# A streaming Huber loss: three pairs of 32 KiB-per-partition tiles replaced by two pairs of 48 KiB-per-partition tiles

## The chip, the core and the metric

The kernel runs on one core of one Trainium2 chip. The metric is the device time of one execution in microseconds (us); lower is better. Beside the times of repeated executions there is a profile of one execution, with a record of every instruction on every engine and of every packet that the core's 16 DMA engines moved. Engine names are those of the profile: DVE is VectorE, ACT is ScalarE, POOL is GpSimd, and SP is SyncE, which here only issues transfers ("SPq" is its instruction queue).

## The reference

Two fp32 matrices of 8192 x 8192 go in and one of the same size comes out. Every element is computed by itself:

```python
def reference(pred, target):
    delta = 1.0
    diff = pred - target
    abs_diff = np.abs(diff)
    return np.where(abs_diff <= delta, 0.5 * diff**2, delta * (abs_diff - 0.5 * delta))
```

There is no reduction and no reuse: 256 MiB of `pred` and 256 MiB of `target` are read once, 256 MiB are written once, 805.3 million bytes in all.

## The kernel before

**Tiling.** The 8192 rows are cut into 64 blocks of 128 rows. In block `i` each of the 128 partitions holds one row of 8192 fp32 elements, which is 32 KiB per partition and 4 MiB per transfer. A tile `a` receives `pred`, a tile `b` receives `target`, and the result is computed in place: `a` ends up holding the output and is the source of the store. Three pairs of `a` and `b` rotate (`DEPTH = 3`), 6 x 32 = 192 KiB per partition.

**Arithmetic.** The whole tile is loaded by two transfers, but computed in four pieces of 2048 columns. For one piece, `first` issues two DVE instructions (the difference `a = a - b`, line 58; the difference clipped to -1..1 into `b`, line 59) and three ACT instructions (`a = |a|`, line 62; `a = relu(a - 1)`, line 63; `b = b*b`, line 64). `second` issues one more DVE instruction (`a = 0.5*b + a`, line 69). Since ACT needs what DVE made and line 69 needs what ACT made, a piece's `second` is put into DVE's order two pieces later: a list `late` holds the pieces that are waiting. The list lives across tiles. So the last two pieces of tile `i` get their `second` only after the `first` of two pieces of tile `i + 1`, and DVE, which runs its instructions in order, can issue those only when tile `i + 1` has landed.

**Order of the transfers.** All transfers are issued by SP, in one program order, on one hardware queue. The order is written out by hand (`manual_schedule` for SP, DVE and ACT). Three tiles are loaded at the start: b, a, b, a, b, a. From then on, when the last `second` of tile `j` has been issued, SP gets the store of tile `j` (line 53) and then the loads of tile `j + 3` into the same pair: `b` (line 49), then `a` (line 50). Three waits follow from the buffers: the store waits for line 69 of the tile's last piece; the load of `b` waits for that tile's compute alone; the load of `a` waits until the store of the same buffer has landed, and everything behind it on SP waits with it.

**End.** The last tile is loaded in two halves (four transfers of 2 MiB) and stored in four pieces of 1 MiB, each as soon as its `second` is through. The tile before it is stored whole.

Of the kernel before, what the change touches and what calls it, by code (L numbers as in the profile page):

```python
# [1 line left out]

# [4 lines left out]

P = 128
ROW = 8192
PIECE = 2048  # L10
DEPTH = 3


@with_exitstack
def kernel(
    ctx: ExitStack,
    tc: tile.TileContext,
    pred: bass.AP,
    target: bass.AP,
    out: bass.AP,  # L20
):
    nc = tc.nc
    f32 = mybir.dt.float32
    Alu = mybir.AluOpType
    Act = mybir.ActivationFunctionType
    Eng = mybir.EngineType

    pred_t = pred.rearrange("(n p) m -> n p m", p=P)
    targ_t = target.rearrange("(n p) m -> n p m", p=P)
    out_t = out.rearrange("(n p) m -> n p m", p=P)  # L30
    n = pred_t.shape[0]
    H = ROW // 2

    const = ctx.enter_context(tc.tile_pool(name="const", bufs=1))
    pool_a = ctx.enter_context(tc.tile_pool(name="pool_a", bufs=DEPTH))
    pool_b = ctx.enter_context(tc.tile_pool(name="pool_b", bufs=DEPTH))

    neg1 = const.tile([P, 1], f32)
    nc.vector.memset(neg1, -1.0)  # L39

    A, B = {}, {}

    def load(i, halves):


        A[i] = pool_a.tile([P, ROW], f32, name="a")
        B[i] = pool_b.tile([P, ROW], f32, name="b")
        for lo, hi in halves:
            nc.sync.dma_start(out=B[i][:, lo:hi], in_=targ_t[i, :, lo:hi])  # L49
            nc.sync.dma_start(out=A[i][:, lo:hi], in_=pred_t[i, :, lo:hi])  # L50

    def store(i, lo, hi):
        nc.sync.dma_start(out=out_t[i, :, lo:hi], in_=A[i][:, lo:hi])

    def first(i, lo, hi):

        a, b = A[i][:, lo:hi], B[i][:, lo:hi]
        nc.vector.tensor_tensor(out=a, in0=a, in1=b, op=Alu.subtract)  # L58
        nc.vector.tensor_scalar(  # L59
            out=b, in0=a, scalar1=-1.0, scalar2=1.0, op0=Alu.max, op1=Alu.min  # L60
        )
        nc.scalar.activation(out=a, in_=a, func=Act.Abs)  # L62
        nc.scalar.activation(out=a, in_=a, func=Act.Relu, bias=neg1)  # L63
        nc.scalar.activation(out=b, in_=b, func=Act.Square)  # L64

    def second(i, lo, hi):

        a, b = A[i][:, lo:hi], B[i][:, lo:hi]
        nc.vector.scalar_tensor_tensor(  # L69
            out=a, in0=b, scalar=0.5, in1=a, op0=Alu.mult, op1=Alu.add  # L70
        )

    whole = [(0, ROW)]
    split = [(0, H), (H, ROW)]
    pieces = [(lo, lo + PIECE) for lo in range(0, ROW, PIECE)]

    with tc.manual_schedule(engines={Eng.SP, Eng.DVE, Eng.Activation}):
        for i in range(DEPTH):
            load(i, whole)
        late = []  # L80
        for i in range(n):
            for k, (lo, hi) in enumerate(pieces):
                first(i, lo, hi)
                late.append((i, lo, hi))
                if len(late) > 2:
                    j, l, h = late.pop(0)
                    second(j, l, h)
                    if h == ROW and j < n - 1:
                        store(j, 0, ROW)
                        if j + DEPTH < n:  # L90
                            load(j + DEPTH, split if j + DEPTH == n - 1 else whole)
                    elif j == n - 1:
                        store(j, l, h)
        for j, l, h in late:
            second(j, l, h)
            store(j, l, h)


# [1 line left out]
_INS = ['pred', 'target']  # L100
_OUTS = [((8192, 8192), 'float32')]


# [23 lines left out]
```

## Time and profile before

| What | Value |
|---|---|
| Median of 3 executions | 1875.93 us (1875.44 to 1877.06) |
| The profiled execution's own time | 1875.44 us |
| Its span in the profile | 1873.7 us |
| DVE busy | 1446.7 us, 77% of the span |
| ACT busy | 1447.2 us, 77% of the span |
| Transfers of SP's queue | 805.32 MB, their packets fill 99.9% of the 16 engines' span |
| Mean rate | 430 GB/s |
| Transfers issued | 189 of 4 MiB, 4 of 2 MiB, 4 of 1 MiB |

How to read it: the span runs from the first to the last record of the profiled execution and is 1.7 us shorter than its time. "Busy" is the time in which an engine executed something, not what an engine could do. The share of the DMA queue is the time that its packets took, divided by 16 engines' spans. A rate over a slice of the span is the bytes of the packets in it over its length. In groups of instructions, the idle time is that of the engine just before the instruction, with the releaser that ended it.

### The profile page before, as it was taken

The page shows a single profiled execution, that of the slowest core. Times are in us where ns is not written, and L with a number is a line of the kernel's source. Part 1 is how long each engine was busy: PE and PEld are TensorE (multiplying, and loading weights), DVE is VectorE, ACT ScalarE, POOL GpSimd, SP SyncE. Part 2 cuts the span into 40 slices and gives each one's busy share as a digit, 9 for nine tenths or more (in the row PEclk, how much of TensorE's full clock was granted, in tenths as well). Part 3 has the DMA queues.
Part 4 walks back from the last instruction along what each step waited for, and adds up shares of the span by engine and source line. Part 5 has one row for each costly group of instructions (what it writes and reads, how often), then busy time and mean ns, then how long its engine had stood idle before and what let it go on. Part 6 is the DMA issues. An engine that isn't in the chain of part 4 may idle for free.

```text
span 1873.7 us, 1976 instructions
## 1 busy us (share of the span) xinstructions
DVE 1446.7 (77%) x769; ACT 1447.2 (77%) x769; POOL 0.2 (0%) x4
## 2 busy tenths in 40 slices
DVE  4986877878778778787787877878778787787777
ACT  4986877878778787787877878778778787787877
POOL 0000000000000000000000000000000000000000
DMA  9999999999999999999999999999999999999998
GB/s 414 425 435 430 432 433 432 432 433 432 433 435 430 433 434 431 432 434 432 432 434 431 432 434 432 432 434 432 434 434 431 434 433 432 432 434 434 431 411 373
DMA packets 28384, 805.45 MB, mean 430 GB/s; under 512 B 3152, under 2 KB 3152, under 8 KB 3152
## 3 DMA queue, kind: packets, MB, share of 16 engines
q1 hardware_dynamic: 28368, 805.32, 99.9%
q14 instruction: 16, 0.13, 0.0%
HBM read 536.87 MB, written 268.44 MB: 430 GB/s over the span
## 4 chain that ended last, share of the span: by engine, by line
DMA 74%; DVE 20%; issue 3%; ACT 2%; ACTq 0%; SPq 0%; DVEq 0%
DMA out_dram<-a 44%; DMA a<-in_pred_dram 30%; DVE a L58 8%; DVE a L69 8%; DVE b L59 4%; ACT a L62 1%; ACT b L64 1%; ACT a L63 1%; ACTq L122 0%; DVEq L58 0%; SPq L49 0%; SPq L50 0%
## 5 line engine op out<-in xcount | busy, mean ns | idle before, releaser
L58 DVE TENSOR_TENSOR a<-a,b 128x2048 f32<-128x2048 f32 x256 | 585.2, 2286 | 405.7 <-DMA a<-in_pred_dram 353.9
L62 ACT ACTIVATE a<-a 128x2048 f32<-128x2048 f32 x256 | 488.8, 1909 | 382.9 <-DVE b L59 382.9
L69 DVE SCALAR_TENSOR_TENSOR a<-b,a 128x2048 f32<-128x2048 f32 x256 | 584.8, 2285 | 1.4 <-ACT b L64 1.4
L63 ACT ACTIVATE a<-a,neg_64 128x2048 f32<-128x2048 f32 x256 | 512.5, 2002 | 8.3
L64 ACT ACTIVATE b<-b 128x2048 f32<-128x2048 f32 x256 | 484.7, 1893 | 0.0
L59 DVE TENSOR_SCALAR b<-a 128x2048 f32<-128x2048 f32 x256 | 314.1, 1227 | 8.8
L62 ACT ACT_TABLE_LOAD x1 | 1.3, 1283 | 22.7 <-DMA a<-in_pred_dram 22.7
L39 DVE MEMSET neg_64<- 128x1 f32 x1 | 0.1, 59 | 0.8 <-PEq L111 0.8
L111 POOL MEMSET const-bfloat16-1.0<- 128x1 bf16 x1 | 0.1, 102 | 0.0
L111 POOL MEMSET const-uint8-127<- 128x1 uint8 x1 | 0.1, 102 | 0.0
L111 POOL MEMSET const-float32-1.0<- 128x1 f32 x1 | 0.1, 99 | 0.0
L111 POOL MEMSET const-float32-0.0<- 128x1 f32 x1 | 0.1, 98 | 0.2 <-issue 0.2
## 6 DMA issues: line engine op xcount, KB each, us to landing
b<-in_target_dram SPq DMA_DIRECT2D x63, 4096.0 KB, 36.5
a<-in_pred_dram SPq DMA_DIRECT2D x63, 4096.0 KB, 19.4
out_dram<-a SPq DMA_DIRECT2D x63, 4096.0 KB, 27.2
b<-in_target_dram SPq DMA_DIRECT2D x2, 2048.0 KB, 23.0
a<-in_pred_dram SPq DMA_DIRECT2D x2, 2048.0 KB, 15.0
out_dram<-a SPq DMA_DIRECT2D x4, 1024.0 KB, 10.3
```

What stands on the lines that cost most here:

```text
L39: nc.vector.memset(neg1, -1.0)
L58: nc.vector.tensor_tensor(out=a, in0=a, in1=b, op=Alu.subtract)
L59: nc.vector.tensor_scalar(out=b, in0=a, scalar1=-1.0, scalar2=1.0, op0=Alu.max, op1=Alu.min)
L62: nc.scalar.activation(out=a, in_=a, func=Act.Abs)
L63: nc.scalar.activation(out=a, in_=a, func=Act.Relu, bias=neg1)
L64: nc.scalar.activation(out=b, in_=b, func=Act.Square)
L69: nc.vector.scalar_tensor_tensor(out=a, in0=b, scalar=0.5, in1=a, op0=Alu.mult, op1=Alu.add)
L111: nc = _bacc.Bacc("TRN2", target_bir_lowering=False, num_devices=1)
```

## The change

The two inputs and the output are flattened and cut into contiguous blocks of 128 x 12288 elements: 48 KiB per partition and 6 MiB per transfer. 67,108,864 elements make 42 such blocks and a last one of 128 x 8192, so there are 43 tiles in place of 64. `DEPTH` is 2: two pairs of 48 KiB tiles, 4 x 48 = 192 KiB per partition as before. A piece is still 2048 columns, so a tile has six pieces (the last tile four), and every arithmetic instruction has the shape it had and occurs 256 times.

The list `late` is now made anew for each tile and emptied at the tile's end: all six `second` of tile `i` stand in DVE's order ahead of the first `first` of tile `i + 1`. The store of tile `i` follows them, then the loads of tile `i + 2` into the same pair. The last tile is loaded in two halves of 4096 columns (2 MiB each) and stored in four pieces, as before. SP issues 126 transfers of 6 MiB, 4 of 2 MiB and 4 of 1 MiB, 134 in place of 197. SP's waits are of the same kinds as before.

```diff
-ROW = 8192
+ROW = 12288
 PIECE = 2048
-DEPTH = 3
+DEPTH = 2
...
-    pred_t = pred.rearrange("(n p) m -> n p m", p=P)
-    targ_t = target.rearrange("(n p) m -> n p m", p=P)
-    out_t = out.rearrange("(n p) m -> n p m", p=P)
-    n = pred_t.shape[0]
-    H = ROW // 2
+    total = pred.shape[0] * pred.shape[1]
+    flat = [x.rearrange("r c -> (r c)") for x in (pred, target, out)]
+
+    tiles = []
+    at = 0
+    while at < total:
+        w = min(ROW, (total - at) // P)
+        tiles.append((at, w))
+        at += P * w
+    n = len(tiles)
+
+    def dram(x, i):
+        at, w = tiles[i]
+        return flat[x][at : at + P * w].rearrange("(p m) -> p m", p=P)
...
+    def cuts(w, step):
+        return [(lo, min(lo + step, w)) for lo in range(0, w, step)]
+
-    def load(i, halves):
+    def load(i):
         A[i] = pool_a.tile([P, ROW], f32, name="a")
         B[i] = pool_b.tile([P, ROW], f32, name="b")
-        for lo, hi in halves:
-            nc.sync.dma_start(out=B[i][:, lo:hi], in_=targ_t[i, :, lo:hi])
-            nc.sync.dma_start(out=A[i][:, lo:hi], in_=pred_t[i, :, lo:hi])
+        w = tiles[i][1]
+        for lo, hi in cuts(w, w // 2 if i == n - 1 else w):
+            nc.sync.dma_start(out=B[i][:, lo:hi], in_=dram(1, i)[:, lo:hi])
+            nc.sync.dma_start(out=A[i][:, lo:hi], in_=dram(0, i)[:, lo:hi])
 
     def store(i, lo, hi):
-        nc.sync.dma_start(out=out_t[i, :, lo:hi], in_=A[i][:, lo:hi])
+        nc.sync.dma_start(out=dram(2, i)[:, lo:hi], in_=A[i][:, lo:hi])
...
     with tc.manual_schedule(engines={Eng.SP, Eng.DVE, Eng.Activation}):
         for i in range(DEPTH):
-            load(i, whole)
-        late = []
+            load(i)
         for i in range(n):
-            for k, (lo, hi) in enumerate(pieces):
+            w = tiles[i][1]
+            late = []
+            for lo, hi in cuts(w, PIECE):
                 first(i, lo, hi)
-                late.append((i, lo, hi))
+                late.append((lo, hi))
                 if len(late) > 2:
-                    j, l, h = late.pop(0)
-                    second(j, l, h)
-                    if h == ROW and j < n - 1:
-                        store(j, 0, ROW)
-                        if j + DEPTH < n:
-                            load(j + DEPTH, split if j + DEPTH == n - 1 else whole)
-                    elif j == n - 1:
-                        store(j, l, h)
-        for j, l, h in late:
-            second(j, l, h)
-            store(j, l, h)
+                    second(i, *late[0])
+                    if i == n - 1:
+                        store(i, *late[0])
+                    late.pop(0)
+            for lo, hi in late:
+                second(i, lo, hi)
+                if i == n - 1:
+                    store(i, lo, hi)
+            if i < n - 1:
+                store(i, 0, w)
+                if i + DEPTH < n:
+                    load(i + DEPTH)
```

More of the change, by code (lines that the diff above doesn't have):

```diff
@@ L71, in second @@
         )
-    whole = [(0, ROW)]
-    split = [(0, H), (H, ROW)]
-    pieces = [(lo, lo + PIECE) for lo in range(0, ROW, PIECE)]
     with tc.manual_schedule(engines={Eng.SP, Eng.DVE, Eng.Activation}):
         for i in range(DEPTH):
-            load(i, whole)
-        late = []
+            load(i)
         for i in range(n):
-            for k, (lo, hi) in enumerate(pieces):
+            w = tiles[i][1]
+            late = []
+            for lo, hi in cuts(w, PIECE):
                 first(i, lo, hi)
-                late.append((i, lo, hi))
+                late.append((lo, hi))
                 if len(late) > 2:
-                    j, l, h = late.pop(0)
-                    second(j, l, h)
-                    if h == ROW and j < n - 1:
-                        store(j, 0, ROW)
-                        if j + DEPTH < n:
-                            load(j + DEPTH, split if j + DEPTH == n - 1 else whole)
-                    elif j == n - 1:
-                        store(j, l, h)
-        for j, l, h in late:
-            second(j, l, h)
-            store(j, l, h)
+                    second(i, *late[0])
[10 more added lines that the diff above has]
+                    load(i + DEPTH)
 _INS = ['pred', 'target']
```

## The prediction

> **What bounds the kernel now.** I read the page first: engines, rates and the queue.
>
> ```profile
> span 1873.7 us, 1976 instructions
> DVE 1446.7 (77%) x769; ACT 1447.2 (77%) x769; POOL 0.2 (0%) x4
> ...
> DMA  9999999999999999999999999999999999999998
> GB/s 414 425 435 430 432 433 432 432 433 432 433 435 430 433 434 431 432 434 432 432 434 431 432 434 432 432 434 432 434 434 431 434 433 432 432 434 434 431 411 373
> ...
> q1 hardware_dynamic: 28368, 805.32, 99.9%
> ```
>
> DVE and ACT idle for a quarter of the span, the DMA engines never: 431 to 435 GB/s in nearly every slice. So the transfers are the bound, their bytes stay the same, and only two things can move the time: the rate while the queue is full, and stretches in which it runs empty.
>
> Next the windows of one 4 MiB round each (29.06 us), at the end of the run, where the queue empties:
>
> ```profile
> 1760.49:1789.55 29.06, 22.60 (x13) 22.59 (x13) 0.00 (x0) 1.00 1.00 433
> 1789.55:1818.61 29.06, 22.63 (x13) 22.63 (x13) 0.00 (x0) 1.00 1.00 430
> 1818.61:1847.67 29.06, 28.89 (x16) 28.90 (x16) 0.00 (x0) 1.00 0.96 389
> 1847.67:1868.50 20.83, 14.31 (x8) 13.40 (x8) 0.00 (x0) 1.00 0.97 416
> ```
>
> The last column is GB/s: a full round moves 430 to 433, the last stretches 389 and 416. The loss against 432.5 is 29.06 x 43.5/432.5 + 20.8 x 16.5/432.5 = 3.7 us; on the slowest DMA engine, whose landings decide, the trace has 2.3 us of it.
>
> Then the timeline of all engines over the first tile (start, duration, instruction), and that of SP's queue in a steady stretch.
>
> ```profile
> 0.73 0.38 SPq L49 DMA_DIRECT2D b<-in_target_dram  x1
> ...
> 22.72 2.29 DVE L58 TENSOR_TENSOR a<-a,b 128x2048 f32<-128x2048 f32 x1 [21.86 <-DMA a<-in_pred_dram]
> ...
> 26.31 1.91 ACT L62 ACTIVATE a<-a 128x2048 f32<-128x2048 f32 x1 [2.33 <-DVE b L59]
> ...
> 37.60 1.89 ACT L62 ACTIVATE a<-a 128x2048 f32<-128x2048 f32 x1
> ...
> 53.59 0.35 SPq L53 DMA_DIRECT2D out_dram<-a  x1
> ```
>
> ```profile
> 1705.51 0.33 SPq L50 DMA_DIRECT2D a<-in_pred_dram  x1
> 1707.37 0.34 SPq L53 DMA_DIRECT2D out_dram<-a  x1
> ...
> 1734.59 0.33 SPq L50 DMA_DIRECT2D a<-in_pred_dram  x1
> ```
>
> Line 50 is issued the moment a store lands: 1705.51, 1734.59, so every 29.08 us, 9.69 us per 4 MiB transfer. The first pair lands at 22.7 us; a piece takes ACT 5.64 us (two from 26.31 to 37.60); the first store goes out at 53.59, before the sixth load ends (6 x 9.7 + 3.3 = 61.5). Three pairs keep the queue full from the start.
>
> **The change part by part.** The sum is made against the profiled execution (1875.44 us, span 1873.67) and raised by 0.5 us to the median. All on the slowest DMA engine.
>
> *Bytes and packets.* By the packet records a 32768-byte packet takes 1.213 us, 16384 bytes 0.611, 8192 bytes 0.309: a line of 36.8 ps per byte and 8 ns per packet. Nothing more is visible per transfer: 8 packets per engine are 9.70 us, the landings 9.69 us apart. A 49152-byte packet is then 1.816 us and a 6 MiB transfer 14.51 us. Before: 189 x 9.693 = 1832.0 us. After: 126 x 14.51 = 1828.3. **-3.7 us.** Bounds: 0, if the longer rows bring nothing; -10, if everything ran at the best slice's 435 GB/s (805.3/0.435 = 1851.3 us against 1832.0 + 4 x 4.88 + 4 x 2.43 = 1861.2); +12 at the slices' 430. I take the packet line, measured on the operation itself.
> The Trainium skill speaks here for the change and against it. "SBUF — State Buffer", section "The DMA setup-cost knee", gives each transfer a fixed 2 us or so; 63 fewer would be -126 us and a sum near 1775. The row of landings shows no such cost while the queue is full. "DMA: Bandwidth & Descriptors", section "Where 436 GB/s comes from", sets a ceiling of 435.2 GB/s, by which no transfer size could give more than some 11 us; by it the sum would be 1890 at best.
>
> *The start.* Only two pairs are loaded ahead. The first pair lands 2 x (14.51 - 9.69) = 9.6 us later than 22.7, at 32.3; the second has its last byte in at 61.0 and lands at 61.3. Computing a tile of six pieces: ACT starts 3.59 us after DVE (26.31 - 22.72), works 6 x 5.64 = 33.9, the last line 69 takes 2.29: 39.8 us, and SP issues 0.05 later. So store 0 is issued at 72.2. Its first bytes move 1.1 us after issue (first packets of the run: 1.80 against 0.73), at 73.3. The queue behind it holds only loads that need this store's or this compute's buffers, so all 16 engines stand still from 61.0 to 73.3: **+12.3 us, and 0.7** for slow first packets (1.4 to 2.1 us in place of 1.2 when the queue fills from empty). Nothing hides it: three pairs did. Bounds: 11 (if packets move at once on issue) to 14.5 (2.6 us between issue and landing beyond transfer, 22.72 - 0.73 - 19.39, all of it ahead).
>
> *The steady rounds.* Per tile the transfers take 3 x 14.51 = 43.5 us, the compute 39.8. Counted from the last byte of tile i's `a`: 0.35 to landing (packet end to semaphore), 0.1 to DVE, 39.85, 1.1 to the store's first bytes = 41.4. Tile i+1's last byte is in at 43.5. The store arrives **2.1 us early**, and behind it the next `b` (14.5 us) covers the wait of `a` for the store's landing. So 0. With the whole 2.6 us above taken ahead of the bytes, the margin is 0.9. DVE and SP meanwhile wait in order: no `first` of tile i+1 passes the emptying of `late`, but that tile has not landed anyway.
>
> *The end.* Take E as the last byte of tile 41's `a`. Store 40 (14.5) and the four 2 MiB loads (4 x 4.87) keep the queue until E+34.0. Store 41 waits for tile 41's compute: first bytes at E+41.4, **idle 7.4, and 0.7** to restart; in until E+56.6. Tile 42 starts on DVE at E+40.3. Its `second`s follow the order p0 p1 p2 s0 p3 s1 s2 s3 and ACT's 5.64 us steps: the four stores are issued at E+53, 58.7, 63.2 and 68.8. Each moves 2.43 us, so the queue waits 0.7, 2.1 and 3.2 us more; end at E+72.3, against 58.2 of transfers: **+14.1 us**. Before, three pairs let the last tile's first half land under the compute of the tile ahead, and the same stretch lost 2.3. Net **+11.8**. Bounds: 9 (bytes move at once on issue, which takes 1.1 off, and 3.7 lost before) and 14 (what was lost before is lost again).
>
> *Arithmetic, issues.* The same 256 instructions of each kind by the same rows; 63 fewer issues of 0.4 us on SP, which waits most of the span: 0. Memory stays at 192 KiB per partition.
>
> **Sum:** -3.7 + 13.0 + 11.8 = +21.1: profiled 1896.5, median 1897.0 us, 1.1% slower.
>
> **The rivals.**
>
> 1. *The steady cover is too short.* If the store comes x us after the last byte of the next tile, two tiles share one such chain, so each round grows by x/2; 40 rounds make 20 us per us. For: the margin is only 2.1 us of 43.5, and the landings of one transfer differ by 0.4 us between engines early and up to 6.3 late. Against: the slowest engine's own landing starts the compute and its own queue is what must not run dry; the others idling costs nothing. With x = 1: 1917 us; if half of the 6.3 counted (x = 1): the same; if all of it (x = 4.2): 1981.
>
> 2. *6 MiB blocks stream slower*, for their rows or addresses in memory: at 430 GB/s 15.7 us above my sum (12 + 3.7), 1913. Nothing in the profile speaks for it but the spread of its slices.
>
> 3. *Not slower: longer rows stream faster.* The two gaps cost 24.8 us. To pay for them a 49152-byte packet must save 24.8/1008 = 25 ns against 1.5 x 1.212 us: 1.793 us, 438.6 GB/s. From there on the change isn't slower; at 441 GB/s it would be 1866. Against: no slice of 40 is over 435, and three packet sizes lie on one line. For: no packet of this size is in the trace.
>
> 4. *The rows are not moved as 48 KiB packets* but are cut (32 + 16): the change then doesn't do what it says, and -3.7 becomes 0: 1900.7.
>
> **How the numbers follow.** My forecast together with rival 4: 0.73, its own range 1889 to 1904 from the bounds of its terms. Rival 1: 0.13, mostly 1905 to 1925. Rival 2: 0.06. Rival 3: 0.08, of it 0.05 faster and 0.03 within 0.2% (3.8 us, about what a measurement of this kernel can tell from no change). So slower by over 0.2%: 0.92. The range 1886 to 1916 holds nearly all of the first, half of rivals 1 and 2, and leaves the rest out.
>
> **What would show it.** In the profile after: the DMA share falls in the second of the 40 slices (some 13 of 46.8 us) and in the last two, and stays at 9 between, at 432 to 434 GB/s. SP's first store is issued near 72, its line for `a` every 43.5 us. DVE's wait for `a` is some 3.7 us per tile. ACT and DVE keep their busy sums. Wrong would be: rounds above 44 us with a DMA share below 1 inside them (rival 1), or with a full share (rival 2); rounds under 43.2 (rival 3); about 33300 data packets in place of 17152 (rival 4); or a first store before 65 us.

## The result, and the profile after

The changed kernel takes 1917.91 us (median of four executions, 1916.55 to 1919.87); the kernel before took 1876.49 us in the same comparison. The ratio is 1.0221, 95% interval 1.0203 to 1.0239: **2.2% slower**, 41 us, where 21 us had been forecast.

The page of the changed kernel, the same parts as were shown of before:

```profile
span 1914.8 us, 1891 instructions
...
DVE 1452.6 (76%) x769; ACT 1440.0 (75%) x769; POOL 0.2 (0%) x4
...
DMA  9799999999999999999999999999999999999996
GB/s 416 307 426 429 437 431 428 427 435 418 438 416 428 439 414 438 417 440 419 422 427 430 424 427 428 427 440 414 439 421 437 424 429 426 429 425 419 435 416 279
...
q1 hardware_dynamic: 19296, 805.31, 98.4%
```

DVE and ACT do what they did. The gap at the start (second slice, 307 GB/s) and the one at the end (279) are where the prediction put them. What it did not have is between: the engines are busy in every slice (9), but the rate averages less than the 432 to 433 of before. The swing from 414 to 440 is mostly the page's counting. It puts a packet's bytes whole into the slice in which the packet starts, and 16 packets of 48 KiB are 16 GB/s of a slice of 47.9 us; spread over the packets' times, the records give 423 to 433 in these slices. The windows of the changed kernel by stage say how much is lost (last two columns: DMA share, GB/s):

```profile
0.00:61.00 61.00, 27.79 (x17) 25.51 (x14) 0.20 (x4) 1.00 0.97 413
61.00:74.00 13.00, 7.42 (x4) 9.50 (x6) 0.00 (x0) 1.00 0.14 60
...
134.60:1841.40 1706.80, 1313.40 (x695) 1304.23 (x697) 0.00 (x0) 1.00 1.00 428
1841.40:1875.50 34.10, 31.41 (x17) 30.07 (x17) 0.00 (x0) 1.00 0.93 387
1875.50:1883.50 8.00, 4.66 (x3) 3.66 (x2) 0.00 (x0) 1.00 0.23 98
1883.50:1914.80 31.30, 20.68 (x12) 22.51 (x12) 0.00 (x0) 1.00 0.73 310
```

The kernel before, over its middle and over one stretch of it:

```profile
134.60:1818.60 1684.00, 1304.55 (x694) 1304.37 (x694) 0.00 (x0) 1.00 1.00 432
379.00:1790.00 1411.00, 1091.86 (x580) 1091.45 (x580) 0.00 (x0) 1.00 1.00 433
```

The middle 1707 us of the changed kernel have a DMA share of 1.00 and 428 GB/s. At 432.5 the same bytes would take 1689 us. So some 18 us were lost with the DMA engines busy. SP's queue in the changed kernel shows it from another side, in the steps from store to store (line 66):

```profile
1704.69 0.34 SPq L66 DMA_DIRECT2D out_dram<-a  x1
...
1749.34 0.34 SPq L66 DMA_DIRECT2D out_dram<-a  x1
...
1793.03 0.34 SPq L66 DMA_DIRECT2D out_dram<-a  x1
...
1837.77 0.34 SPq L66 DMA_DIRECT2D out_dram<-a  x1
```

Steps of 44.65, 43.69 and 44.74 us: every second round loses about 1.1 us against the forecast 43.5, and the steps alternate like this through most of the run. Over the run the mean from store to store is 44.16 us (the expectations below say 44.05, read from single rounds).

The packet records say what kind of loss it is. A 48 KiB packet normally takes 1.816 us, as forecast. But 731 of 16128 take over 5% longer, up to 3.3 us in the rounds. I call these *stretched*, and add up what they take beyond the normal in engine-us: 384 over the whole run, 362 of it in packets over 2% long after the first 10 us (before: 52 by the same count). Divided by 16 engines the difference is 19.4 us. That is nearly all of the 20.9 us between forecast and result. They lie at the turns of the queue: some 220 engine-us in the last packet of a store with a load behind it, 28 in the packet before it, 30 in the first packet of that load, 43 in the last two packets of a load with a store behind it, by an assignment of the packets to engines from their times. At one such turn 14 engines' packets start within 0.15 us of each other (1762.94 to 1763.09) and come out 0.5 to 1.1 us too long together. The two slowest engines lose 0.9 and 0.6 us at the next turn, at 1793.

The packet records also say how early the store is for the first engines to arrive, and not only for the slowest. An engine's landing is recorded some 0.4 us after its last byte, and after a real gap a store's first bytes move 0.84 us after its issue. A store that is issued less than about 1.3 us before the first engine's landing of the load ahead is therefore too late for that engine. From 380 us on the rounds fall into two groups. In 18 of 33 the store was issued 0.6 to 1.4 us before that landing; each of these rounds holds 10 to 15 stretched engine-us. In the other 15 it was issued 1.6 to 2.0 us before, and they hold 3 to 7. The pauses themselves are short: by the same assignment three or more engines stop for over 0.1 us in 11 of the 18 rounds, by at most 0.75 us, and in 3 of the 18 none does.

### The profile page after: what moved, and what is told of

Its sections match the earlier page's. It is cut to its first block, busy times and chain, and to the rows that moved or that the text cites. A ratio compares the mean times of both kernels' runs of the same rounds, so it can differ in the third digit from the quotient of the medians.

```text
span 1914.8 us, 1891 instructions
## 1 busy us (share of the span) xinstructions
DVE 1452.6 (76%) x769; ACT 1440.0 (75%) x769; POOL 0.2 (0%) x4
## 4 chain that ended last, share of the span: by engine, by line
DMA 61%; ACT 31%; DVE 6%; issue 1%; ACTq 0%; DVEq 0%; SPq 0%
DMA a<-in_pred_dram 37%; DMA out_dram<-a 25%; ACT a L76 11%; ACT a L75 10%; ACT b L77 10%; DVE a L82 3%; DVE a L71 2%; DVE b L72 1%; ACTq L133 0%; DVEq L71 0%; SPq L62 0%
## 6 DMA issues: line engine op xcount, KB each, us to landing
a<-in_pred_dram SPq DMA_DIRECT2D x42, 6144.0 KB, 29.6
a<-in_pred_dram SPq DMA_DIRECT2D x2, 2048.0 KB, 14.8
```

## The experiments

Three theories could explain stretched packets. LOCKSTEP: they appear where the queue turns from store to load or back while most engines stand at the same packet; a store that is not issued when the leading engines reach it makes them idle and restart together, which keeps them in step. SIZE: packets of 48 KiB do it at every such turn. LATE STORE: a transfer issued shortly before it is needed is itself slow. "Cover" below is the time by which a store is ready before the slowest engine's queue needs it: 2.1 us in the changed kernel by the prediction's working.

### Less work: a large cover (e1)

```diff
-        nc.scalar.activation(out=a, in_=a, func=Act.Relu, bias=neg1)
...
-        nc.vector.scalar_tensor_tensor(
-            out=a, in0=b, scalar=0.5, in1=a, op0=Alu.mult, op1=Alu.add
-        )
+        return
```

> Leaves out the relu on ACT (line 76) and the last DVE step (line 82), so a tile computes in some 26 us in place of 39.8 and every store is ready some 16 us before the queue needs it; transfers, sizes, order and number of pairs are those of the changed kernel. After the change a round of three 6 MiB transfers takes 44.05 us on the slowest DMA engine in place of 43.53, all of it in packets that take longer than 1.816 us (384 engine-us, 24 us per engine), most of them the last packet of a store or the first of the load behind it. Theory LOCKSTEP (packets stretch where a queue turns from store to load or back while the engines stand close together; the late store makes the leading engines idle and restart together, which keeps them close): with no late store the engines spread, rounds fall to 43.55, stretched packets to under 80 engine-us, no gap at the start and little at the end: 1873 us. Theory SIZE (48 KiB packets stretch at every such turn, whatever the cover): rounds stay at 44.05: about 1893 us. Theory LATE STORE (a transfer that is issued just before it is needed is itself slow): as LOCKSTEP, 1873 us.

Measured: 1871.73 us, ratio to before 0.9976 (0.9966 to 0.9987). From store to store 43.58 us, 55 stretched engine-us. Windows of this kernel in an early and a late stretch:

```profile
205.00:379.00 174.00, 82.25 (x49) 86.49 (x49) 0.00 (x0) 1.00 1.00 433
379.00:1790.00 1411.00, 672.91 (x392) 710.80 (x394) 0.00 (x0) 1.00 1.00 433
```

The same transfers run at the full 433 GB/s throughout. SIZE falls. Two pairs of 48 KiB tiles are thus no handicap to the queue when the compute is out of the way, and the landings of 6 MiB transfers come 14.51 us apart, the figure that the prediction drew from the line of packet sizes. The Trainium skill's fixed cost per transfer ("SBUF — State Buffer", section "The DMA setup-cost knee") is again not to be seen in a queue that stays full: by it 63 fewer transfers would be worth 126 us, an estimate; e1 is 4 us faster than the kernel before.

### A cover of 4.6 us (e2)

```diff
-            for lo, hi in cuts(w, PIECE):
+            for lo, hi in pieces(w):    # 1024, 2048 x 5, 1024 columns
```

> All the work of the changed kernel, but the first and the last piece of each tile have 1024 columns in place of 2048 (seven pieces in place of six). ACT starts 1.7 us earlier and the last step ends 1.1 us earlier, so the store's cover grows from 2.1 to about 4.6 us. LOCKSTEP: the leading engines may run up to 4.6 us ahead before they idle; turns are then mostly apart, rounds 43.6 to 43.75, and with 2.6 us less at the start and 3 less at the end 1895 to 1902 us. SIZE: rounds stay at 44.05, only the ends gain: 1912 us. LATE STORE: the store still comes shortly before it is needed, rounds near 43.9: 1906 us.

Measured: 1906.35 us, ratio 1.0156 (1.0139 to 1.0173). That is LATE STORE's figure, but the rounds aren't its rounds (44.07 us from store to store, not 43.9). The windows of this kernel, the same two stretches:

```profile
205.00:379.00 174.00, 137.33 (x84) 137.26 (x84) 0.00 (x0) 1.00 1.00 433
379.00:1790.00 1411.00, 1098.60 (x672) 1098.09 (x672) 0.00 (x0) 1.00 1.00 429
```

Up to 379 us nothing is lost, with stores as late for the slowest engine as ever after; then the loss sets in. In between, the landings of one transfer drifted apart between the first and the last engine, from 2.1 us (at 206 us) to 3.6 (at 382) and 4.5 (at 558). The store's issue came ever closer to the first engine's landing of the load ahead: 3.6 us before it at 202 us, 2.1 at 378, 1.5 at 509, 0.9 at 598, with 1, 2, 7 and 11 stretched engine-us in these rounds. When the lead of the fast engines has used up the cover, they reach the store's turn as the store arrives, and from then on the loss is close to that of the changed kernel. Here too the pauses are short: three or more engines stop for over 0.1 us in 7 of 33 rounds. My own expectation under LOCKSTEP (43.6 to 43.75) was wrong: I had taken the spread from first to last engine for what matters. It is large here, 4.2 to 4.6 us, but made by a few stragglers; the first eight engines land within 0.1 to 0.4 us, against 0.7 to 0.9 in the late rounds of the kernel before.

### 4 MiB transfers with a short cover (e3)

```diff
-ROW = 12288
+ROW = 8192
...
-            for lo, hi in cuts(w, PIECE):
+            for lo, hi in pieces(w):    # 1024, 2048 x 3, 1024 columns
```

> The changed kernel with tiles of 8192 columns: 4 MiB transfers and 32 KiB packets as before the change, but two pairs, and pieces of 1024, 2048, 2048, 2048, 1024 columns, so that the store's cover is 1.5 us of a round of 29.08, as short as after the change. Gap at the start 9 us, some 5 us more than before at the end. SIZE: 32 KiB packets don't stretch, rounds 29.08 to 29.15: about 1890 us. LOCKSTEP and LATE STORE: the turns stretch with packets of this size too, about 0.5 us a round over 62 rounds: rounds 29.5 to 29.6, about 1920 us.

Measured: 1909.29 us, ratio 1.0180 (1.0161 to 1.0199); 29.46 us from store to store, 364 stretched engine-us; 427 GB/s from 379 to 1790 us. Packets of 32 KiB, which before the change ran at 433, stretch as soon as the cover is short. It is less than I expected (29.5 to 29.6), but 19 us off SIZE's figure.

### Three pairs, restarted together (e4)

```diff
+        if i % 8 == 7 and i < 60 and lo == 0:
+            for _ in range(30):
+                nc.vector.tensor_scalar(
+                    out=b, in0=b, scalar1=-1.0, scalar2=1.0, op0=Alu.max, op1=Alu.min
+                )
```

> The kernel before the change, with 30 more clips of b (each leaves b as it is, 1.15 us) ahead of ACT's work on the first piece of tiles 7, 15, 23, 31, 39, 47 and 55. Each makes the stores some 28 us late, so that the queue runs empty for 11 to 13 us once and all engines restart together; two or three rounds later three pairs have the stores issued far ahead again. Total about 1955 to 1975 us, from the gaps. LOCKSTEP: in the four to six rounds behind each gap packets stretch as in the first 190 us of the run before (there the slowest engine lost about 4 us and 38 engine-us in all), 15 to 40 engine-us per gap, also in rounds in which the store is issued over 8 us ahead of its turn, and the spread of the landings falls to under 1 us at each gap and grows again. LATE STORE: stretched packets only in rounds whose store was late; none once it is 8 us ahead. A third theory, COLD START (what slowed the first 190 us of the run before happens once, at the first use of memory): no stretched packets behind the gaps.

Measured, a single execution: 2053.54 us. The gaps were larger than I had worked out, some 22.7 us each in place of 11 to 13; that carries no weight here. What counts is what follows a gap. Windows of this kernel, the first gap and the rounds behind it, and its queue:

```profile
248.00:260.00 12.00, 11.86 (x9) 4.26 (x3) 0.00 (x0) 1.00 0.00 0
260.00:271.94 11.94, 11.87 (x7) 11.88 (x7) 0.00 (x0) 1.00 0.99 395
271.94:301.10 29.16, 28.98 (x16) 29.00 (x16) 0.00 (x0) 1.00 0.99 415
...
447.10:476.30 29.20, 22.51 (x15) 22.32 (x12) 0.00 (x0) 1.00 1.00 433
```

```profile
259.81 0.34 SPq L53 DMA_DIRECT2D out_dram<-a  x1
...
282.47 0.34 SPq L53 DMA_DIRECT2D out_dram<-a  x1
...
305.11 0.34 SPq L53 DMA_DIRECT2D out_dram<-a  x1
```

The store issued at 282.47 has its turn only when the load ahead of it lands at 292.2: it is some 9 us early. Yet this round, 271.94 to 301.10, is the one that runs at 415 GB/s, with 14.7 stretched engine-us. The next five rounds have 3.1, 3.2, 2.5, 3.9 and 2.1 though their stores are issued some 17 us ahead, the one after 0.5, the one after that none. The spread of the landings fell from 3.0 to 0.4 us at the gap and grew back over these rounds. So a common restart stretches packets with stores in good time, which LATE STORE alone can't explain, and it does so anew after a gap in mid-run, which COLD START can't. All seven gaps show it: the restarting store's own stretch has 14.8 to 17.4 stretched engine-us, the round after it, with its store early, 10.7 to 15.6.

DVE and ACT catch up in that round (29 us busy of 29.16), so full compute beside the transfers is a rival here. But 14.5 of its 14.7 engine-us lie in the last two packets of the one load ahead of the early store, and none in the packets between the turns. The kernel before shows the same once, at its own start: its first loads follow one another closely in step (the first eight engines land within 0.18 us), nothing is stretched from 10 to 58 us, and then 10.7 engine-us fall on the last packets ahead of the first store, which had been issued 8 us before its turn.

The sizes agree in part. In the changed kernel the rounds in which the store arrives with the first engines have 10 to 15 engine-us, like the two stretches above; the rounds between them have only 3 to 7.

### A mended cover with all the work: halves of both inputs (e6), and of a alone (e8)

```diff
-        for lo, hi in cuts(w, w // 2 if i == n - 1 else w):
+        for lo, hi in cuts(w, w // 2):
```

> The changed kernel with every tile loaded in halves, b, a, b, a of 6144 columns, 3 MiB and 24 KiB packets, as the last tile already is; compute, stores and number of pairs as after the change. The first three pieces can start when half a tile has landed, so a store is ready some 16 us before its turn, and the gaps at both ends go. LOCKSTEP and LATE STORE: rounds 43.6 to 43.75 (24 KiB packets cost 8 ns more each, 5.4 us in all): 1875 to 1880 us. If something other than the store's cover stretched the packets (the two pairs themselves, or full compute beside the transfers, which e1 had not): rounds stay near 44.1 and the time near 1898.

Measured: 1879.41 us, ratio 1.0019 (1.0009 to 1.0028); 65 stretched engine-us, 43.79 us from store to store. The compute is whole and there are two pairs; the loads are cut in halves, the cover is long, and the loss is gone.

```diff
+            if i == n - 1:
+                nc.sync.dma_start(out=B[i][:, lo:hi], in_=dram(1, i)[:, lo:hi])
+            elif lo == 0:
+                nc.sync.dma_start(out=B[i][:, :w], in_=dram(1, i))
             nc.sync.dma_start(out=A[i][:, lo:hi], in_=dram(0, i)[:, lo:hi])
```

> The changed kernel with only a loaded in halves (b whole), so the store's cover is some 9.4 us in place of 2.1, with all the work done. LOCKSTEP: a cover beyond the 6.3 us that the engines spread to by themselves is never used up, so the leaders never idle and never restart together: rounds 43.55 to 43.7, gap at the start 5.8 in place of 13, at the end some 7 us: 1882 to 1889 us. If the cover merely has to be used up later: rounds 43.55 at first and 44.1 from some point on, as in e2 from 420 us: 1890 to 1902 us.

Measured: 1887.85 us, ratio 1.0063 (1.0048 to 1.0078); 62 stretched engine-us. The windows of this kernel run the other way round from e2's:

```profile
47.00:94.00 47.00, 41.18 (x23) 40.92 (x23) 0.00 (x0) 1.00 0.89 375
...
205.00:379.00 174.00, 134.87 (x72) 133.58 (x73) 0.00 (x0) 1.00 1.00 431
379.00:1790.00 1411.00, 1100.28 (x582) 1089.90 (x583) 0.00 (x0) 1.00 1.00 433
```

The engines came together at the gap at the start, lost a little, and drifted apart: 0.5 us at 105 us, 3.5 at 500, 7.3 at 1800. With 9.4 us of cover the store was issued at least 3.6 us before the first engine's landing up to 1780 us, so the leaders never met an empty queue, and the rate stayed at 433. The stores and the loads of b are still transfers of 6 MiB. Compared with e2 (4.6 us: lost from 379 us on), this brackets what the cover must exceed here: the drift that the engines reach by themselves.

### The two ends alone (e7)

```diff
-        for lo, hi in cuts(w, w // 2 if i == n - 1 else w):
+        for lo, hi in cuts(w, w // 2 if i in (0, n - 2, n - 1) else w):
```

> The changed kernel with only tiles 0 and 41 loaded in halves (the last one is anyway): store 0 is ready at 57.7 us, before the second pair's last byte at 61, and store 41 before the last tile's loads are in. Both gaps go (13.3 us at the start, some 12 at the end), the 40 rounds between keep the cover of 2.1 us. LOCKSTEP: rounds stay at 44.05: 1917.9 - 25 = 1893 us. If the stretched packets come from the restart after the gap at the start (all engines aligned once, then for good): rounds 43.6 and 1875 us.

Measured: 1899.27 us, ratio 1.0122 (1.0105 to 1.0139). The windows of this kernel:

```profile
61.00:74.00 13.00, 11.69 (x7) 8.14 (x5) 0.00 (x0) 1.00 1.03 442
...
379.00:1790.00 1411.00, 1085.72 (x575) 1075.37 (x575) 0.00 (x0) 1.00 1.00 427
```

The gap at the start is gone and the rounds lose what they lost (427 GB/s, 44.20 us from store to store), so it is not that one gap which sets the engines in step for good: each short cover does it again. Of the end I had expected too much. Tile 41 lands half a tile earlier, but DVE and ACT are on tile 40 until 1826 us, so store 41 still leaves the queue empty for 2.5 us, and the four last stores for 5.9 in all.

### A cover below zero (e5)

```diff
-PIECE = 2048
+PIECE = 4096
```

> The changed kernel with pieces of 4096 columns (three per tile). The chain from a tile's last byte to its store's first byte grows from 41.4 to some 47 us, 3.5 us beyond a round of 43.53: the store is late on every engine. By the prediction's first rival a round then takes (43.53 + 47)/2 = 45.3 us, if the idle time covers the stretched packets, and 45.8 if they come on top; gap at the start 19 us, at the end some 8 us more. 1980 to 2005 us.

Measured, a single execution: 1958.32 us, below what I expected. Longer instructions cost less per column (three ACT steps of 4096 columns take 10.9 us, two pieces of 2048 take 11.28), so the chain is 45.4 us and not 47. By the formula of the first rival a round is then (43.53 + 45.4)/2 = 44.5 us. This kernel's queue:

```profile
928.83 0.34 SPq L66 DMA_DIRECT2D out_dram<-a  x1
...
974.28 0.34 SPq L66 DMA_DIRECT2D out_dram<-a  x1
...
1018.56 0.34 SPq L66 DMA_DIRECT2D out_dram<-a  x1
...
1064.03 0.34 SPq L66 DMA_DIRECT2D out_dram<-a  x1
```

Two rounds take 89.7 to 89.8 us, 44.9 each: 0.4 above the formula, and 0.5 below a full chain of 45.4 in every round. There are some 540 stretched engine-us (34 us per engine, 0.8 a round), so idle time may hide part of them. The halving of the price fits; it isn't shown to better than this.

### Small tiles at the end (e9)

```diff
-        w = min(ROW, (total - at) // P)
+        left = (total - at) // P
+        w = ROW if left > 20480 else {20480: 8192, 12288: 6144, 6144: 4096, 2048: 2048}[left]
...
-            if i == n - 1:
+            if i in (0, n - 1):
```

The diff is against e8.

> The kernel with a in halves (cover 9.4 us, 1887.9 us, rounds 43.6), with b of tile 0 in halves too, and the last 20480 columns cut into tiles of 8192, 6144, 4096 and 2048 columns in place of 12288 and 8192. LOCKSTEP and the sum of the prediction for the ends: the gap at the start (5.8 us) goes, and of the 7 us or so at the end all but 1 to 3, with the rounds unchanged: 1874 to 1878 us, level with the kernel before; 2.7 us of it are the 8 ns per packet of the halved rows. If the small tiles at the end are each late with their store, since their loads are short too: 1880 to 1886 us.

Measured: 1888.14 us, ratio 1.0065 (1.0052 to 1.0079), no better than e8 and above both figures that I had expected. The windows of this kernel:

```profile
47.00:94.00 47.00, 39.26 (x21) 40.95 (x23) 0.00 (x0) 1.00 1.00 431
...
1780.00:1820.00 40.00, 34.21 (x19) 33.98 (x19) 0.00 (x0) 1.00 0.85 355
...
1860.00:1887.00 27.00, 10.31 (x6) 13.63 (x8) 0.00 (x0) 1.00 0.56 209
```

The gap at the start is gone as expected (431 GB/s where e8 had 375), but the end lost what the start gained. A small tile's loads are over before the large tile ahead of it is computed: from 1780 to 1820 us the queue already runs dry. No version with all the work beat the kernel before.

## Why the prediction was wrong

*The start* held. Store 0 was issued at 72.9 (forecast 72.2); the second pair landed at 62.0 on the slowest engine and store 0 at 89.8, 13.3 us more than its 14.5 (forecast 13.0). The queue stood empty for 12.1 us (forecast 12.3). Both pairs landed 0.7 us later than forecast, which cancels in the gap; the store's first bytes moved 0.84 us after its issue in place of 1.1. (The 1.1 was read a little too long: the first packets of the run before start at 1.73 and not at 1.80.)

*The end* held. From the landing of tile 41's `a` (1841.53) to the last landing (1913.83) it took 72.3 us, as forecast from E to the end. The queue stood empty for 6.6 us ahead of store 41 (forecast 7.4) and for 1.0, 1.9 and 3.0 us ahead of the last three stores (0.7, 2.1 and 3.2).

*Bytes and packets* held: 14.51 us per 6 MiB transfer in e1, and undisturbed 48 KiB packets at 1.816 us.

*The steady rounds* failed. The cover of 2.1 us was worked out rightly (2 to 4 us by the packet records): in the changed kernel the slowest engine did not run dry (its stores land 14.5 to 14.7 us after the load ahead, hardly more than the 14.5 that they take). The step that failed is "So 0", and under it a sentence of the first rival, that the other engines' idling costs nothing. The lead of the fast engines, which the rival had read off (up to 6.3 us late in the run before), is larger than the cover. So the store arrives late or only just in time for them, and holds the leaders together; where they meet a turn of the queue together, their packets stretch. That the cover is what decides is shown: e1, e6 and e8 lengthen it and the loss goes, e2 lengthens it less and the loss comes later, e3 shortens it with smaller transfers and the loss appears. That it works by holding the engines in step is the best supported reading (e2's onset, e4's restarts), but not proved for every round. The slowest engine's packets stretch too, though it never waited. In place of 0 the term measures 0.6 us per round, some 25 us over 40 rounds; some 3 us of stretched packets (52/16) were in the run before as well, which leaves about the 20.9 us that the sum of 1897.0 lacked.

The first rival got the place right, a cover that is too short for the spread of the engines, and the size by luck: its 1917 us came from idling on the slowest engine with x = 1, which did not happen. Its formula for real idling is met within 0.4 us a round by e5. The second rival (6 MiB blocks stream slower) named a symptom that came true, full share and rounds above 44 us; e1 rules out the cause that it gave. The third and the fourth did not come about: no faster packets, and 17152 packets with data, as forecast, against some 33300, had the rows been cut.

What stays open is what in the chip stretches the packets. Being in step isn't enough without a turn between directions: five loads of the run before follow one another with the first eight landings within 0.18 us, and the four of the changed kernel with 0.44 us, and nothing is stretched. A turn in step isn't always enough either: behind e4's first gap the turn from store to load at 302 us, with the first eight landings within 0.31 us, has 0.2 stretched engine-us. Whether the memory, the path to it or the engines' own handling of the queue is the place, no run here tells. That a store which arrives just in time adds something of its own beside the common restart is not excluded: some rounds of the changed kernel and of e2 stretch by 10 engine-us and more with no pause over 0.1 us on any engine.

## What to carry to other kernels

When a transfer queue is the bound, as here, work out for each buffer scheme by how much every transfer is queued ahead of its turn, and compare that with the spread of one transfer's landings over the engines, not with zero. Fewer and larger tiles in the same memory shorten this cover, since the whole tile must be computed before its store. Loading each tile in halves gives it back at a few us. Price the first load and the last store of a larger tile too: they were 25 us here and could be worked out from the timeline to within a microsecond.

## What the runs showed of the hardware that was not expected

- With the DMA share at 1.00 the rate still differed by 1.2% (428 against 433 GB/s). A share says that packets were under way, not that they moved at full rate; the durations of equal packets tell the two apart.
- The 16 engines drift apart by themselves in a queue that never runs dry, and that is the state in which it runs at full rate: from 0.4 to 6.3 us over the run of the kernel before, 1.1 to 5.7 in e1, 0.5 to 7.3 in e8. Common idling resets it, to 0.4 us in e4.
- A common restart costs some 3 us per engine: 45 stretched engine-us from e4's first gap on (14.8 up to the landing of the restarting store and 14.7 in the round behind it), 41 to 51 from each of its seven gaps to the next.
- The packets stretch where the queue turns between loads and stores, and hardly anywhere else: some 320 of the changed kernel's 362 engine-us lie in the packets next to such a turn that are listed above.
